# Stores of memory keys and output gates on the sync queue, seven staging tiles for keys, and a tail pool cut into parts

## The chip, the cores and the metric

The kernel runs on one core of a Trainium2 chip. A core has five engines, each with its own instruction queue: TensorE (PE in the profile, with weight loads listed as PEld), VectorE (DVE), ScalarE (ACT), GpSimd (POOL) and SyncE (SP), which here only issues DMA transfers. ScalarE issues transfers too; the issues are listed as SPq and ACTq. The metric is the device time of one execution in microseconds (us).

## The reference, cut to what matters

One layer of a bidirectional encoder on a sequence of 2048 rows of width 1024, with 256 memory rows. All of it is float32:

```python
u = rms_norm(h); proj = u @ w_in                     # columns for hyena, q k, v, o, gates
hy = short_conv(proj[..., :1536])                    # width 3, centred
qk = silu(short_conv(proj[..., 1536:2560]))          # width 3, centred
y_hy = group_rms_norm(hyena(hy), 8)                  # 512 channels, long filters by FFT
y_ml = group_rms_norm(sigmoid(o) * mlstm(qk, v, gates), 4)   # 4 heads x 128, both directions
h = h + concat(y_hy, y_ml) @ w_out
x, m = rms_norm(h), rms_norm(mem)                    # mem: 256 rows
h = h + softmax((x @ xa_wq) @ (m @ xa_wk).T / 16) @ (m @ xa_wv) @ xa_wo   # by 4 heads of 256
h = h + relu(rms_norm(h) @ ff_w1) ** 2 @ ff_w2
out = rms_norm(h)
```

## The kernel before, in words

A float32 product is written as three products of a high and a low part: `mm3` (lines 357, 360, 361) multiplies high by high, low by high and high by low. `split` (line 368) makes the parts: the high one by a cast on ScalarE, the low one by a subtraction on VectorE.

The program runs in stages that are woven into each other. Up to some 1020 us the rows of x are normalised and projected (`sweep`), the Hyena filters are transformed and the first Hyena products run. `sweep` writes each block of 128 rows by 256 columns by a copy or a sigmoid into a staging tile "st" (3 tiles in turn) and stores it: values into `vd`, output gates into `od` (line 886, on ScalarE's queue). From some 1020 to 1185 us `memproj` prepares the cross-attention: the product of the key weights with the memory is multiplied by the query weights (`keys`, L709 to L718), and the values by the output weights (`values`, L720 to L730). Each result goes from PSUM by ScalarE into a staging tile "o" (the same three "st" tiles, L706), and from there to DRAM: 16 stores of keys `gd` (L718) and 32 of values `vw` (L730), 256 KB each, all issued by ScalarE. The end of the Hyena part (loads `a<-zg`, `a<-hy`, stores `yh<-a`) and the first chunks of the mLSTM (loads `qn`, `kk_t`, `va`, `cbn`, `kn`, `og`; products L1188, L1272, L1310, L1312; normalised rows stored as `ym`) run beside it.

Attention follows from some 1190 to 1700 us, woven with the other mLSTM chunks: for each of four blocks of 512 rows it loads the rows of `yh` and `ym` (L1452), turns them with TensorE (L1458), splits them into `act`, multiplies with the columns of `w_out` (L1383, weights `wh`, `wl`; the first columns go through tiles "we"), adds the rows of x (`acc`, L1485), and then goes on with the keys `gd` and values `vw`. The feed-forward part follows to the end.

Memory on the chip is given out in pools. `i_sb` holds what the input and Hyena stages need, the staging tiles among it; it is closed before attention, and `tail_open` puts one pool `t` in its place with the residual `acc`, the activations, the weights and four loading tiles "wn". A tile of a new pool waits for the work on whatever lay in the same place of a pool that is closed.

The order on each engine is made by a scheduler when the program is built, from the order in which the generators are woven; it is fixed when the kernel runs. Each transfer that SP or ScalarE issues gets one of eight completion semaphores in turn, common to both queues, so an issue waits for the landing of the transfer that had it before, eight transfers back. In the profile a wait of this kind is listed as a wait for the tile of that other transfer.

## Time and profile before

| | us |
|---|---|
| median of 3 runs | 3109.32 (3107.85 to 3111.45) |
| the profiled execution | 3110.14 |
| its span | 3108.4 |
| TensorE busy in the span | 3025.3 |

The granted clock of TensorE over the profiled execution is 0.99 of full speed. A row of a list of waits reads: engine and line, what it waited for, total, times, longest. A row of the timeline reads: start, duration, engine, line, operation, tiles with their shapes, and in brackets the idle time before it with what ended it. The tile names are those of the program: `wm` are weights of the memory projection, `o` and `kt` copies out of PSUM, `we` and `wn` loaded weights or rows, `ht` the output of a chunk.

### The profile page before, as it was taken

Reading aid. Unit: us, or ns where it says so; the run is one execution under the profiler, and the core shown is the slowest. Engines: PE = TensorE matmul, PEld = TensorE weight load, DVE = VectorE, ACT = ScalarE, POOL = GpSimd, SP = SyncE. Lnnn points to the kernel's source line nnn. Section 1 sums busy time; section 2 is a strip of 40 time slices with the busy share of each in tenths; the row PEclk is TensorE's granted clock in tenths of the full one; section 3 lists DMA queues with packets and bytes.
Section 4 is the critical chain, followed back from the end, with each engine's and each line's share of the span. In section 5 each row is a group of like instructions: output and inputs, shape, how many; then the busy total and the mean of one; then the engine's idle time right before and its main releaser. Section 6 shows DMA issues by size and latency. Waiting matters only on the chain.

```text
span 3108.4 us, 42926 instructions
## 1 busy us (share of the span) xinstructions
PE 3025.3 (97%) x14257; PEld 2374.5 (76%) x14257; DVE 1955.3 (63%) x3429; ACT 1497.7 (48%) x2931; POOL 1141.1 (37%) x802
## 2 busy tenths in 40 slices
PE   8999999999999998999999999999999999999998
PEld 6655667776676766888887888888888788888876
DVE  7865465446756456877664566657554676565696
ACT  6543466533656225565544455556555443333335
POOL 0122011200222333333132337766466375243693
PEclk9999999999999999999999999999999999999999
DMA  6654768576878996565476557657644565354435
GB/s 211 190 198 163 231 207 251 178 232 194 254 203 241 302 300 220 158 199 170 143 250 206 197 172 235 207 178 238 200 153 153 171 210 182 109 166 118 157 93 172
DMA packets 444102, 607.07 MB, mean 195 GB/s; under 512 B 38494, under 2 KB 248542, under 8 KB 442856
## 3 DMA queue, kind: packets, MB, share of 16 engines
q1 hardware_dynamic: 405988, 546.54, 55.2%
q10 hardware_dynamic: 37892, 57.79, 5.5%
q8 instruction: 113, 1.85, 0.2%
q14 instruction: 109, 0.89, 0.1%
HBM read 401.79 MB, written 202.41 MB: 194 GB/s over the span
## 4 chain that ended last, share of the span: by engine, by line
PE 55%; DVE 3%; DMA 1%; issue 1%; ACT 1%; POOL 0%; SPq 0%; DVEq 0%; POOLq 0%; ACTq 0%
PE mm L361 12%; PE mm L357 12%; PE mm L360 12%; PE hy L357 6%; PE hy L361 6%; PE hy L360 6%; DVE bl L1668 1%; PE hy L1310 1%; PE hy L1312 1%; DVE acc L1960 0%; PE hy L1458 0%; DVE acc L1994 0%; PE hy L1571 0%; DMA va<-vd 0%; PE hy L1272 0%
## 5 line engine op out<-in xcount | busy, mean ns | idle before, releaser
L1668 DVE TENSOR_TENSOR bl<-wr,bh 128x512 fp32r<-128x512 f32 x213 | 242.1, 1142 | 127.6 <-ACT bh L1667 122.9
L1667 ACT CAST ah<-w 128x512 fp32r<-128x512 f32 x284 | 176.5, 622 | 301.1 <-PE hy L360 155.9
L368 DVE TENSOR_TENSOR wl<-wn,wh 128x512 fp32r<-128x512 f32 (+1 forms) x296 | 213.1, 765 | 101.0 <-ACT wh L368 100.4
L357 PE MATMUL mm<-xh,wh 128*128 128x512 f32 x640 | 267.5, 419 | 8.5 <-ACT wh L368 7.9
L1024 POOL TENSOR_TENSOR b<-b,a 128x512 f32<-128x512 f32 x64 | 87.0, 1362 | 509.4 <-ACT b L1022 238.8
L360 PE MATMUL mm<-xl,wh 128*128 128x512 f32 x640 | 253.7, 397 | 1.3 <-DVE xl L368 1.3
L361 PE MATMUL mm<-xh,wl 128*128 128x512 f32 x640 | 254.8, 399 | 0.0
L1667 ACT CAST bh<-wr 128x512 fp32r<-128x512 f32 x232 | 143.5, 621 | 230.2 <-PE mm L361 172.6
L1668 DVE TENSOR_TENSOR al<-w,ah 128x512 fp32r<-128x512 f32 x236 | 216.0, 916 | 55.5 <-ACT ah L1667 54.1
L357 PE MATMUL mm<-bh,ah 128*128 128x512 f32 x576 | 225.2, 391 | 1.8 <-DVE acc L1830 1.7
L361 PE MATMUL mm<-bh,al 128*128 128x512 f32 x576 | 223.3, 390 | 2.6 <-POOL al L1668 2.6
L360 PE MATMUL mm<-bl,ah 128*128 128x512 f32 x576 | 224.4, 390 | 0.0
L368 ACT CAST wh<-wn 128x512 fp32r<-128x512 f32 (+1 forms) x296 | 164.2, 618 | 109.4 <-PE mm L361 52.7
L360 PE MATMUL mm<-act,wh 128*128 128x512 f32 x512 | 202.3, 395 | 0.0
L361 PE MATMUL mm<-act,wl 128*128 128x512 f32 x512 | 200.5, 393 | 0.9 <-DVE wl L368 0.9
L357 PE MATMUL mm<-act,wh 128*128 128x512 f32 x512 | 199.6, 396 | 1.3 <-ACT wh L368 1.2
L357 PE MATMUL hy<-bh,ah 128*128 128x512 f32 x448 | 175.2, 391 | 0.0
L360 PE MATMUL hy<-bl,ah 128*128 128x512 f32 x448 | 174.6, 390 | 0.0
L361 PE MATMUL hy<-bh,al 128*128 128x512 f32 x448 | 174.4, 390 | 0.0
L357 PEld LDWEIGHTS mm<-xh,wh 128*128 128x128 f32 x640 | 121.1, 189 | 60.8 <-issue 18.6
L357 PE MATMUL mm<-wh,xh 128*128 128x256 f32 (+1 forms) x512 | 156.0, 305 | 3.8 <-ACT xh L368 2.3
L361 PEld LDWEIGHTS mm<-xh,wl 128*128 128x128 f32 x640 | 121.0, 189 | 47.8 <-issue 23.2
(375 smaller groups left out, 8225.4 us busy)
## 6 DMA issues: line engine op xcount, KB each, us to landing
wr<-hc SPq DMA_DIRECT2D x224, 256.0 KB
w<-in_ff_w_dram SPq DMA_DIRECT2D x172, 256.0 KB
hc<-wn SPq DMA_DIRECT2D x128, 256.0 KB
wn<-in_w_in_dram SPq DMA_DIRECT2D x100, 256.0 KB
hc<-q SPq DMA_DIRECT2D x96, 256.0 KB
fs<-a SPq DMA_DIRECT2D x32, 512.0 KB
a<-fs SPq DMA_DIRECT2D x64, 256.0 KB
a<-zs SPq DMA_DIRECT2D x64, 256.0 KB
```

What stands on the lines that cost most here:

```text
L357: first = mm(ps, lh, rh, start=start, stop=False)
L360: mm(ps, lh, rl, start=False, stop=False)
L361: self.last = mm(ps, ll, rh, start=False, stop=stop)
L368: both = (self.nc.scalar.copy(hi, src), self.nc.vector.tensor_tensor(lo, src, hi.bitcast(F32), ALU.subtract))
L1024: nc.gpsimd.tensor_tensor(xt, xt, hi[:, m], ALU.mult)
L1310: nc.tensor.matmul(dst, nm[:, h], va[:, h], start=True, stop=state is None)
L1312: nc.tensor.matmul(dst, rows_[d, 1][:, h], state[:, h], start=False, stop=True)
L1667: self.nc.scalar.copy(hi, src)
L1668: eng.tensor_tensor(lo, src, hi.bitcast(F32), ALU.subtract)
```

## The change

The change has four parts. The input pool is cut in three, `i_w` (tiles "cv" and "wn"), `i_st` (the three "st") and the rest, and the tail pool in four, which lie over them one by one: `t_w` (the first pair of weights), `t_acc` (`acc`), `t` (one pair of activations, the second pair of weights) and `t_n` (the other activations and the loading tiles). The staging of keys takes the three "st" tiles and the four "wn" tiles by turns. The 16 stores of keys, and 16 of the 32 stores of output gates, are issued by SP. And one chunk of the mLSTM fewer is written ahead of attention; attention's first two steps and two of the mLSTM are written by turns before the two are woven as before.

```diff
+        sw = self.isw = es.enter_context(tc.tile_pool(name="i_w", bufs=1))
+        for tag, n, bufs in (("cv", 1088, 2), ("wn", 544, 4)):
+            for _ in range(bufs):
+                sw.tile([128, n], F32, tag=tag, name=tag, bufs=bufs)
+        self.ist = es.enter_context(tc.tile_pool(name="i_st", bufs=1))
         sb = self.isb = es.enter_context(tc.tile_pool(name="i_sb", bufs=1))
...
-        def staged(p):
-            o = sb.tile([128, 2, 256], F32, tag="st", name="o", bufs=3)
+        def staged(p, wide=False):
+            if wide:
+                o = self.isw.tile([128, 2, 256], F32, tag="wn", name="o", bufs=4)
+            else:
+                o = self.ist.tile([128, 2, 256], F32, tag="st", name="o", bufs=3)
             nc.scalar.copy(o, p)
...
-                nc.scalar.dma_start(out=gd[h // 2, :, 2 * i2:2 * i2 + 2, cs], in_=staged(p))
+                nc.sync.dma_start(out=gd[h // 2, :, 2 * i2:2 * i2 + 2, cs], in_=staged(p, i2 % 2 == 0))
...
-                nc.scalar.dma_start(out=(self.d_vd if c2 < 2 else self.d_od)[r0:r0 + 128, 256 * (c2 % 2):256 * (c2 % 2) + 256],
-                                  in_=so)
+                (nc.sync if c2 == 2 else nc.scalar).dma_start(
+                    out=(self.d_vd if c2 < 2 else self.d_od)[r0:r0 + 128, 256 * (c2 % 2):256 * (c2 % 2) + 256], in_=so)
...
     def tail_open(self, es):
-        T = self.T = es.enter_context(self.tc.tile_pool(name="t", bufs=1))
-        self.acc = T.tile([128, 8, 512], F32, name="acc")
+        def pool(name):
+            return es.enter_context(self.tc.tile_pool(name=name, bufs=1))
+
+        self.wp = [pool("t_w"), None]
+        for tag in ("wh", "wl"):
+            self.wp[0].tile([128, 8, 256], F32R, tag=tag, name=tag)
+        self.acc = pool("t_acc").tile([128, 8, 512], F32, name="acc")
+        self.wp[1] = self.ap = pool("t")
         self.acts = 2
         for _ in range(2):
             self.act_tile("act")
         for tag in ("wh", "wl"):
-            for _ in range(2):
-                T.tile([128, 8, 256], F32R, tag=tag, name=tag, bufs=2)
-        self.acts = 0
+            self.wp[1].tile([128, 8, 256], F32R, tag=tag, name=tag)
+        self.T = pool("t_n")
+        self.acts = self.wps = 0
...
+    def pair(self, names):
+        pool = self.wp[self.wps % 2]
+        self.wps += 1
+        return [pool.tile([128, 8, 256], F32R, tag=t, name=n) for t, n in zip(("wh", "wl"), names)]
...
-                             p.turned_in(), take(n, 2), beside_each(n, take(m, 5)))
+                             p.turned_in(), take(n, 2), beside_each(n, take(m, 4)))
...
                 g = p.attention(at)
+                for x in (g, m, g, m):
+                    next(x)
                 weave(g, m, 440, 112, True)
```

The numbers of instructions on TensorE, VectorE and GpSimd stay as they are; 32 transfers go from ScalarE to SP. The line numbers of the changed kernel are 8 to 17 higher than those of the kernel before from the staging of keys on. In the rows that follow, a number at the end (x2) counts like instructions in a row.

ScalarE's queue among the keys, before: each copy of a product (L706) has its store behind it, and brm (a scale of the Hyena part) and kt (the next projected weights) stand among them.

```order
L718 DMA gd<-o 128x2x256
L213 ACTIVATE brm<-ms,eps 128x16
L701 COPY kt<-mm 128x512
L706 COPY o<-mm 128x512
L718 DMA gd<-o 128x2x256
L706 COPY o<-mm 128x512
```

The sync queue at the same place, after: the stores stand between the Hyena loads and stores and the weights wm.

```order
L1064 DMA yh<-a 64x1024 x2
L726 DMA gd<-o 128x2x256
L417 DMA wm<-in_xa_wq_t_dram 128x1024 x2
L969 DMA a<-zg_2628 128x1024 x2
L972 DMA a<-hy 64x1024 x2
L417 DMA wm<-in_xa_wv_dram 128x4x256 x2
L726 DMA gd<-o 128x2x256 x2
L1064 DMA yh<-a 64x1024 x2
```

On ScalarE only the copies, brm and kt are left; every store is now one of the issues that the loads behind it on SP wait for.

The sync queue at the start of attention, before: the first columns of w_out (we) are asked for early, then chunk loads, then the four row loads (wn<-yh), and va and the residual acc behind them.

```order
L1383 DMA we<-in_w_out_dram 128x2x256 x2
L1166 DMA kn<-kn 128x512
L1166 DMA og<-od 128x512
L1346 DMA ym<-ht 128x512 x2
L1247 DMA qn<-qt 128x4x128
L1247 DMA kk_t<-kt 128x4x128
L1172 DMA va<-vd 128x4x128
L1247 DMA cbn<-cbd 128x516
L1166 DMA kn<-kn 128x512
L1452 DMA wn<-yh 128x512 x4
```

The same queue after.

```order
L1469 DMA wn<-yh 128x512 x4
L1401 DMA we<-in_w_out_dram 128x2x256 x2
L1255 DMA cbn<-cbd 128x516
L1180 DMA va<-vd 128x4x128
L1174 DMA kn<-kn 128x512
L1401 DMA we<-in_w_out_dram 128x2x256 x2
L1502 DMA acc<-in_x_t_dram 128x4x512 x2
L1174 DMA og<-od 128x512
L1255 DMA qn<-qt 128x4x128
L1255 DMA kk_t<-kt 128x4x128
L1354 DMA ym<-ht 128x512 x2
L1180 DMA va<-vd 128x4x128
```

The row loads now come first, the weights behind them, and the second va load stands behind the two acc loads and the two ym stores.

VectorE at the start of attention, before: the low parts of the weights (wl), then the denominators (den) of the chunk that TensorE waits for.

```order
L1282 TENSOR_TENSOR rw<-rw,hy 128x512 x2
L1263 STREAM_SHUFFLE rw<-rows_9569 128x512 x2
L368 TENSOR_TENSOR wl<-we,wh 128x512 x3
L1173 MEMSET va 128x4
L1263 STREAM_SHUFFLE rw<-rows_9569 128x512 x2
L368 TENSOR_TENSOR wl<-we,wh 128x512
L1318 TENSOR_TENSOR den<-hy,cols 128x4 x2
L1319 RECIPROCAL den<-den 128x4 x2
```

After: a chunk's output (L1334) stands between the low parts, and the normalisation of a pair of chunks (from L216 on, ending in L1352 further down) right behind them.

```order
L368 TENSOR_TENSOR wl<-we,wh 128x512
L1334 SCALAR_TENSOR_TENSOR ht<-hy,den,ht 128x128 x4
L368 TENSOR_TENSOR wl<-we,wh 128x512 x3
L216 TENSOR_SCALAR hy<-brm 128x8
L218 COPY bry<-hy 128x8
L219 TENSOR_TENSOR hy<-hy,bry 128x8
L220 SCALAR_TENSOR_TENSOR hy<-hy,brm 128x8
```

The denominators no longer stand behind all four low parts, but the normalisation does.

More of the change, by code (lines that the diff above doesn't have):

```diff
@@ L390, in weights @@
                     cs = slice(c0, c0 + 512)
-                    nat = pool.tile([128, 512], F32, tag="wn", name="wn", bufs=nbufs)
+                    nat = self.isw.tile([128, 512], F32, tag="wn", name="wn", bufs=nbufs)
                     nc.sync.dma_start(out=nat, in_=w[128 * k0:128 * k0 + 128, cs])
@@ L395, in weights @@
         for k0 in range(0, kt, kc):
-            nat = pool.tile([128, kc, n], F32, tag="wn", name="wn", bufs=nbufs)
+            nat = self.isw.tile([128, kc, n], F32, tag="wn", name="wn", bufs=nbufs)
             nc.sync.dma_start(out=nat, in_=w[128 * k0:128 * (k0 + kc), :].rearrange("(k p) c -> p k c", p=128))
@@ L465, in square_sum @@
     def square_sum(self, x, dst):
-        junk = self.isb.tile([128, 512], F32, tag="st", name="junk", bufs=3)
+        junk = self.ist.tile([128, 512], F32, tag="st", name="junk", bufs=3)
         return self.tc.keep_in_program_order(self.nc.scalar.activation(junk, x, AF.Square, accum_out=dst))
@@ L530, in room @@
                 return None
-            t = self.isb.tile([128, 1088], F32, tag=("P", "cv")[n % 2], name="xt", bufs=2)
+            t = (self.isb, self.isw)[n % 2].tile([128, 1088], F32, tag=("P", "cv")[n % 2], name="xt", bufs=2)
             return t[:, 0:D].rearrange("p (k t) -> p k t", k=2)
@@ L578, in squares @@
             for k in range(8):
-                sq = sb.tile([128, 512], F32, tag="st", name="sq", bufs=3) if k else ssum[c]
+                sq = self.ist.tile([128, 512], F32, tag="st", name="sq", bufs=3) if k else ssum[c]
                 pin(nc.scalar.activation(sq, xs[k], AF.Square))
@@ L611, in second @@
             for k in range(0, 8, 2):
-                nat = sb.tile([128, 2, 256], F32, tag="wn", name="wn", bufs=4)
+                nat = self.isw.tile([128, 2, 256], F32, tag="wn", name="wn", bufs=4)
                 nc.sync.dma_start(out=nat, in_=wsrc1[:, k:k + 2])
@@ L787, in leave @@
                         ct = 2 * c2 + m
-                        cv = sb.tile([128, 1088], F32, tag="cv", name="cv", bufs=2)
+                        cv = self.isw.tile([128, 1088], F32, tag="cv", name="cv", bufs=2)
                         v = cv[:, 0:n]
@@ L835, in sweep_out @@
             pt = self.mm().rearrange("p (k t) -> p k t", k=4)
-            st = sb.tile([128, 4, 128], F32, tag="st", name="st", bufs=3)
+            st = self.ist.tile([128, 4, 128], F32, tag="st", name="st", bufs=3)
             full = min(4, (n - b) // 128)
@@ L880, in natural @@
                 self.pop()
-                so = sb.tile([128, 512], F32, tag="st", name="st", bufs=3)[:, 0:256]
+                so = self.ist.tile([128, 512], F32, tag="st", name="st", bufs=3)[:, 0:256]
                 if c2 < 2:
@@ L1369, in act_tile @@
         self.acts += 1
-        return self.T.tile([128, 8, 512], F32R, tag=f"act{(self.acts - 1) // 2 % 2}", name=name, bufs=2)
+        return (self.ap if (self.acts - 1) // 2 % 2 else self.T).tile([128, 8, 512], F32R, tag="act", name=name, bufs=2)
+    def pair(self, names):
+        pool = self.wp[self.wps % 2]
+        self.wps += 1
+        return [pool.tile([128, 8, 256], F32R, tag=t, name=n) for t, n in zip(("wh", "wl"), names)]
     def act(self):
@@ L1375, in columns @@
     def columns(self, w, stage=None):
-        hi = self.T.tile([128, 8, 256], F32R, tag="wh", name="wh", bufs=2)
-        lo = self.T.tile([128, 8, 256], F32R, tag="wl", name="wl", bufs=2)
+        hi, lo = self.pair(("wh", "wl"))
         n = 512 // w.shape[2]
@@ L1685, in ffn_x @@
     def ffn_x(self, i, src):
-        nc, T = self.nc, self.T
+        nc = self.nc
         eng = (nc.vector, nc.gpsimd)
@@ L1691, in ffn_x @@
         if i in (7, 3):
-            hi, lo = (T.tile([128, 8, 256], F32R, tag=t, name="x" + t[1], bufs=2).rearrange("p (k n) c -> p k (n c)", n=2)
-                      for t in ("wh", "wl"))
+            hi, lo = (t.rearrange("p (k n) c -> p k (n c)", n=2) for t in self.pair(("xh", "xl")))
         else:
```

11 lines of the change are left out of this document (5 added, 6 removed).

## The prediction

> **What bounds the kernel now.** First the page, for each engine's share of the span.
>
> ```profile
> span 3108.4 us, 42926 instructions
> PE 3025.3 (97%) x14257; PEld 2374.5 (76%) x14257; DVE 1955.3 (63%) x3429; ACT 1497.7 (48%) x2931; POOL 1141.1 (37%) x802
> ```
>
> TensorE works for all but 83.1 us. The change adds and removes no matmul, so all that it can win lies in those 83 us and in the stretches in which TensorE ran below full clock. Second, therefore, a table by stretches, cut where the change moves work: stretch, length, busy time of PE, PEld, DVE, ACT and POOL, granted clock, DMA share, GB/s. The last two rows are the slow-clock pieces of the stretch 1190 to 1220.
>
> ```profile
> 1060.00:1080.00 20.00, 15.62 (x55) 11.39 (x56) 6.74 (x21) 2.84 (x6) 4.38 (x3) 0.83 1.04 339
> 1080.00:1100.00 20.00, 20.00 (x95) 14.89 (x94) 10.52 (x31) 3.13 (x6) 5.69 (x5) 1.00 1.06 369
> 1100.00:1130.00 30.00, 25.09 (x108) 18.87 (x107) 14.03 (x40) 5.64 (x15) 12.22 (x9) 0.89 1.05 348
> 1130.00:1180.00 50.00, 49.80 (x221) 32.43 (x219) 26.82 (x92) 22.18 (x72) 18.96 (x15) 1.00 0.74 246
> 1190.00:1220.00 30.00, 16.95 (x90) 15.37 (x89) 22.48 (x63) 17.30 (x63) 9.45 (x8) 0.77 0.81 268
> 1330.00:1350.00 20.00, 15.60 (x80) 12.81 (x79) 14.09 (x32) 14.73 (x45) 1.60 (x2) 0.83 0.53 151
> 1350.00:1690.00 340.00, 339.83 (x1733) 286.65 (x1732) 229.38 (x524) 176.54 (x451) 96.22 (x70) 1.00 0.57 188
> ...
> 1197.05:1203.87 6.82, 2.94 (x13) 2.94 (x14) 5.25 (x16) 2.30 (x8) 4.20 (x3) 0.51 1.07 373
> 1207.35:1214.20 6.85, 5.05 (x22) 4.95 (x23) 6.57 (x23) 3.72 (x7) 0.00 (x0) 0.50 0.68 224
> ```
>
> Three places lose time: A (1060 to 1130, the keys of the memory projection), B (1190 to 1220, the handover to attention) and C (1330 to 1350, inside attention). Between 1350 and 1690 nothing can be won. A loses 4.38 + 4.91 = 9.3 us idle and by the clock 20 x 0.17 + 30 x 0.11 = 6.7 us more: 16.0 us. B loses 13.05 us idle and half of the 7.99 us that it was busy at half clock, 4.0 us: 17 us. C loses 20 - 15.60 = 4.4 us idle and up to 20 x 0.17 = 3.4 us by the clock.
>
> Third, who waits in A: the waits of TensorE, of ScalarE and of the sync queue from 1020 to 1140 (total, times, longest).
>
> ```profile
> PE mm L716 <- ACT o L706: 3.4, 2, 3.1
> PE mm L716 <- ACT kt L701: 2.4, 1, 2.4
> PE mm L699 <- ACT o L706: 2.0, 1, 2.0
> PE hy L1310 <- DVE a L1052: 1.8, 1, 1.8
> ...
> ACT o L706 <- DMA wm<-in_xa_wq_t_dram: 11.9, 3, 7.6
> ACT o L706 <- DMA wm<-in_xa_wo_dram: 10.1, 1, 10.1
> ...
> SPq L1056 <- DMA a<-zg: 7.8, 4, 3.0
> ```
>
> TensorE waits for ScalarE's copies out of PSUM, and ScalarE waits for loads that its copies never read: a store on ScalarE's queue must have its completion semaphore back from the transfer eight issues earlier, and that was a weight load on the sync queue. The timeline of the longest case, and two rows for the lead of the sync queue over TensorE:
>
> ```profile
> 1094.58 0.59 ACT L706 COPY o<-mm 128x512 f32<-128x512 f32 x1
> ...
> 1104.78 0.37 ACTq L718 DMA_DIRECT2D gd<-o  x1
> 1105.24 0.59 ACT L706 COPY o<-mm 128x512 f32<-128x512 f32 x1 [10.07 <-DMA wm<-in_xa_wo_dram]
> ...
> 1105.88 8.36 PE L716 MATMUL mm<-kt,wm 128*128 128x256 f32 x24 [3.07 <-ACT o L706]
> ...
> 1083.11 0.80 SPq L961 DMA_DIRECT2D a<-zg  x2
> ...
> 1097.22 0.64 PE L178 MATMUL hy<-a,e 128*64 128x512 f32 x1
> ...
> 1041.54 7.07 PE L716 MATMUL mm<-kt,wm 128*128 128x256 f32 x32
> ```
>
> The copy at 1094.58 was done at 1095.2, its store left at 1104.78, and the next copy, for which TensorE stood, came behind it.
>
> Fourth, B: the timelines of the queues and engines from 1164 to 1214, in the order of the argument.
>
> ```profile
> 1179.37 0.37 ACTq L730 DMA_DIRECT2D vw<-o  x1
> ...
> 1186.63 0.41 ACTq L730 DMA_DIRECT2D vw<-o  x1
> ...
> 1192.17 2.18 ACT L368 CAST wh<-we 128x512 fp32r<-128x512 f32 x4 [0.30 <-DMA vw<-o]
> ...
> 1200.28 1.12 ACT L1324 ACTIVATE ht<-hy,den 128x128 f32<-128x128 f32 x4
> ...
> 1204.09 1.28 ACT L1182 ACTIVATE ve<-va,cols 128x129 f32<-128x129 f32 x4 [2.69 <-DMA va<-vd]
> ...
> 1164.65 2.06 SPq L1383 DMA_DIRECT2D we<-in_w_out_dram  x2
> ...
> 1192.09 1.75 SPq L1452 DMA_DIRECT2D wn<-yh  x4
> ...
> 1195.99 1.36 SPq L1172 DMA_DIRECT2D va<-vd  x1
> ...
> 1177.72 2.22 DVE L1344 SCALAR_TENSOR_TENSOR ht<-ht,hy,gml 128x128 f32<-128x128 f32 x8
> ...
> 1193.27 3.70 DVE L368 TENSOR_TENSOR wl<-we,wh 128x512 fp32r<-128x512 f32 x3
> ...
> 1198.15 1.46 DVE L368 TENSOR_TENSOR wl<-we,wh 128x512 fp32r<-128x512 f32 x1
> ...
> 1200.93 2.09 PE L1188 MATMUL hy<-ve,kn 128*128 128x129 f32 x8 [7.58 <-ACT ht L1324]
> ...
> 1209.15 1.12 PE L1458 MATMUL hy<-ident,wn 128*128 128x128 f32 x4 [4.30 <-DVE act L368]
> ```
>
> The last vw store leaves at 1186.63 and has landed by 1192.09, 5.5 us later; only then does the one tail pool open, since it overlies the staging tile of that store. So the row loads start at 1192.09 and the first weight cast at 1192.17, though the weights were asked for at 1164.65. The four low parts hold VectorE from 1193.27 to 1199.6 and stand ahead of the state chunk's denominators: TensorE waits 7.58 us. Behind the blocked row loads the next va load leaves only at 1195.99; ve and then ScalarE's casts of the turned rows follow it: another 4.30 us.
>
> **The change, part by part.** *The 16 gd stores to the sync queue, seven staging tiles for three.* ScalarE loses 16 x 0.37 = 5.9 us of issue and, what counts, the 22.0 us for which its copies stood behind stores. The sync queue gains the 5.9 us and, for each store, a wait for its copy; behind it there stand the hyena loads (a<-zg, a<-hy), yh and the wm weights, and their reader is TensorE. What covers this is the lead: a row of a<-zg left at 1083.11 for a product at 1097.22, 14.1 us ahead. With seven tiles a copy waits for the landing of the store seven back, not three. If nothing else came, all of A's 16.0 us would return. But A runs at the limit of its transfers: DMA share 1.04 to 1.06. The stretch 1060 to 1130 moved 339 x 20 + 369 x 20 + 348 x 30 = 24.6 MB; at the best rate of the table, 369 GB/s, that takes 66.7 us, so with the same bytes inside it, only 3.3 us return. Loads may slide into 1130 to 1180 though, where 246 GB/s left room, and that by up to the lead. Between 3.3 and 16.0 I take the middle, 10 us: the lead of 14.1 us is of the size of the gap, but not all loads have it.
>
> The Trainium skill's page "DMA: Bandwidth & Descriptors", section "Issuing engines are not separate DMA queues", says that transfers issued from different engines run interleaved on the same 16 DMA engines, so that spreading them over issuers saves just the issue time. By that rule the move would be worth no more than the issue time, which lies beside other work here. The trace agrees on the shared engines (share over 1) but shows 22.0 us of waiting on ScalarE besides the issue; whether that returns, no run here shows yet.
>
> *The 16 od stores to the sync queue.* They are issued in the input sweeps, before 1020, where TensorE waits for none of them: 16 x 0.37 us on a queue that waits for its transfers anyway. Zero; ends -1 and +2.
>
> *The pools in parts, and the first turns between chunks 3 and 4.* By the changed order the row loads no longer stand behind va and kn of the next chunks, and their staging tiles no longer overlie those of the vw stores; they wait only for completion semaphores, and leave when the third-last vw store has landed, which in this trace is 1179.37 + 5.5 = 1184.9 instead of 1192.09. That is the gain. The price: the four weight loads, which left from 1164.65 on before, now stand behind the row loads. Four row loads take 1.75 us to issue; the first weights leave at 1186.6 and, with the same 5.5 us, are there at 1192.1: the first cast stays where it was. The second pair stands behind a kn load, and the third cast behind ve. The casts are then spread out and VectorE is done with the low parts some 3 us sooner. But behind them there now stand, on both engines, the sums (junk, brm), the 13 small steps of the normalisation and the 2.22 us of L1344, and TensorE's next chunk waits for these and for the ym store of the same tile, which takes another 5.5 us to land; the va load of chunk 4 comes behind that store. 3 us sooner, then 2.22 + 5.5 = 7.7 us more in the chain, against some 5 us less since the row loads, the turns and the acc loads are out of the way. I put B at 0. Ends: -12 (both waits, 7.58 + 4.30, gone) and +8 (the 7.7 us come on top).
>
> *C.* The row that waits there:
>
> ```profile
> 1335.85 2.10 PE L1458 MATMUL hy<-ident,wn 128*128 128x128 f32 x8 [4.40 <-DMA wn<-yh]
> ```
>
> The loads of the second column block's rows wait for four staging tiles that the low-part casts free; they have that wait in the changed order too. Zero, ends -4.4 and +4.4 (the wait gone, or doubled, since chunks and loads come at other places).
>
> *The feed-forward part*, from 1710, has the same rows in the same order: zero.
>
> **The sum.** The profiled execution took 3110.14 us, 1.7 us more than its span and 0.8 us over the median of 3109.32. 3109.3 - 10 (A) + 0 (B) + 0 (C) = 3099.3; I say 3099. One measurement of this kernel can tell some 0.2%, 6.2 us, from no change.
>
> **Rivals.** *The sync queue becomes the bound in A (slower).* Each of the 16 stores costs it 0.37 us and at most one product's time of waiting for its copy, 7.07 / 4 = 1.77 us: 34.2 us. Less the lead of 14.1 us, hyena's products would be late by up to 20.1 us, with none of A won; half of it, 10 us, gives 3119. It decides from (14.1 - 5.9) / 16 = 0.51 us of extra waiting for each store. For it speaks that this queue already waits for transfers nearly all the time (the row of 7.8 us is one of many); against it, that those waits and the stores' are for the same landings and do not add up.
>
> *The transfers bound A whoever issues them.* Then 3.3 us return: 3106. For it: the share over 1. Against it: the room after 1130. That is also the case in which the change does not do what it says. The rule of the Trainium skill's page quoted above speaks for a time near this one.
>
> *The handover's chain grows by its 7.7 us*, and A's 10 us are nearly eaten: 3109.3 - 10 + 8 = 3107. For it: the order; against it: the loads in front are fewer.
>
> *Both places empty out*: 3109.3 - 16 - 12 = 3081. For it: each wait named here hangs on the one thing removed. Against it: something is always late next, and DMA at its limit in A.
>
> **How the numbers follow.** My forecast, with its own range of 3092 to 3103, gets 0.42; both places empty 0.12; the transfers as bound 0.15; the longer handover 0.11; the sync queue as bound 0.20. The range from 3083 to 3119 leaves out about half of the first and half of the last of these rivals, 0.16. Faster by over 0.2% (under 3103.1): nearly all of the forecast, the empty case and a little of the two small ones, 0.56. Within 0.2%: most of those two, 0.22. Slower: the sync queue, and some of a worse handover, 0.22.
>
> **What would show it.** Right: from 1060 to 1130 no wait of TensorE for o or kt, no slow clock there, ScalarE without waits for wm; row loads of yh ahead of the last vw store's landing; the wait for ht at the handover replaced by one of about the same size for the normalisation, or for va. Wrong: TensorE waiting for a<-zg, a<-hy or wm in A (the sync queue), TensorE still idle there with DMA share at 1.05 (transfers), idle time in B over 20 us or under 6 us, a new wait between 1350 and 1710 for the vw or w_out weights, whose loads then stand closer to those of the feed-forward part.

## The result: slower, where a gain was forecast

| | before, us | after, us |
|---|---|---|
| median of 6 runs each | 3110.36 (3107.85 to 3111.58) | 3124.02 (3118.88 to 3129.37) |
| the profiled execution | 3110.14 | 3129.37 |
| its span | 3108.4 | 3127.6 |

The ratio is 1.0045 (1.0033 to 1.0057): the change costs 13.7 us. The profiled execution is the slowest of its six, 5 us over their median, so of its 19.2 us over the profiled execution before some 14 are the change. The page of the changed kernel, shares of the span:

```profile
span 3127.6 us, 42953 instructions
PE 3031.2 (97%) x14257; PEld 2377.3 (76%) x14257; DVE 1954.8 (63%) x3429; ACT 1501.8 (48%) x2931; POOL 1144.1 (37%) x802
```

The stretches of the changed kernel, in the columns of the table of before (length, busy PE, PEld, DVE, ACT, POOL, granted clock, DMA share, GB/s):

```profile
1060.00:1080.00 20.00, 19.11 (x85) 14.47 (x83) 10.94 (x32) 4.42 (x9) 6.67 (x6) 1.00 1.06 346
1080.00:1100.00 20.00, 16.82 (x75) 12.11 (x76) 7.45 (x19) 2.27 (x5) 4.68 (x4) 0.91 1.06 328
1100.00:1130.00 30.00, 30.00 (x134) 21.75 (x131) 14.16 (x38) 4.61 (x9) 11.30 (x8) 1.00 1.04 363
1130.00:1180.00 50.00, 45.51 (x178) 28.35 (x176) 21.11 (x66) 19.44 (x58) 16.40 (x13) 0.93 0.77 244
1190.00:1220.00 30.00, 20.79 (x117) 18.52 (x116) 24.66 (x73) 16.05 (x58) 12.14 (x10) 0.74 0.68 225
1220.00:1330.00 110.00, 103.04 (x575) 89.15 (x574) 86.75 (x246) 62.87 (x203) 39.57 (x30) 0.98 0.50 154
1350.00:1690.00 340.00, 328.79 (x1639) 275.84 (x1638) 228.94 (x514) 170.77 (x438) 89.91 (x63) 0.98 0.55 177
...
1184.70:1205.20 20.50, 10.54 (x45) 9.81 (x46) 14.54 (x50) 9.86 (x36) 6.29 (x5) 0.50 0.75 259
```

The loss among the keys (1060 to 1130) fell from 16.0 us to 4.07 idle + up to 1.8 by the clock. But 1130 to 1180, which lost 0.2 us, now loses 4.49 idle + up to 3.5 by the clock; 20.5 us of the handover run at half clock; and 1350 to 1690, full before, is idle for 11.2 us.

Since work slides between fixed stretches, the account below is cut at products instead: for each stage, the idle time between TensorE's matmuls, plus half of the time that matmuls ran at half clock, worked out from all the matmuls of the trace. Half, because matmuls in a row start twice as far apart there (the products mm<-mt,wm of the kernel after every 427 ns instead of 216).

| lost, us | before | after |
|---|---|---|
| keys (first key product to first value product) | 15.9 | 6.1 |
| values (to the last value product) | 0.2 | 6.1 |
| handover (to attention's first product act by wh) | 17.7 | 21.5 |
| rest of attention's first block | 0.3 | 8.6 |
| second block | 6.7 | 5.7 |
| third block and fourth block's turns | 0.0 | 10.2 |
| all other stages | 40.9 | 38.7 |
| sum | 81.7 | 96.9 |

15.2 of the 19.2 us stand in it. The keys won 9.8 us. The values and the handover gave that back (+5.9, +3.8), and the first and the third block added 8.3 and 10.2. The account is of the slowest execution, so its sizes are somewhat above those of the medians.

TensorE's waits of the changed kernel, first from 1020 to 1175 and then from 1175 to 1260 (total, times, longest):

```profile
PE hy L178 <- DMA a<-zg: 3.4, 2, 3.1
PE hy L1196 <- ACT ht L1332: 3.3, 1, 3.3
PE mm L724 <- DMA wm<-in_xa_wq_t_dram: 0.9, 2, 0.5
PE mm L704 <- ACT o L714: 0.4, 1, 0.4
...
PE hy L1318 <- ACT rw L1289: 5.6, 1, 5.6
PE hy L1318 <- DVE ht L1352: 5.1, 2, 3.6
PE hy L1318 <- DVE hy L220: 4.2, 1, 4.2
PE hy L1280 <- DVE act L368: 3.3, 2, 1.9
PE hy L1196 <- ACT ht L1332: 2.7, 1, 2.7
```

The waits for o and kt among the keys are all but gone (0.4 us). In their place TensorE waits 3.4 us for a<-zg and 0.9 us for wm, small, but the sign that the prediction had named for its rival of the sync queue. In the second list every wait is one of an mLSTM chunk (L1196, L1280, L1318), for the normalisation (L220, L1352), for ht, for rw and for the low parts of act.

The wait of 3.3 us for ht lies among the values. The timeline of the changed kernel there, ScalarE and TensorE:

```profile
1131.62 0.38 ACTq L738 DMA_DIRECT2D vw<-o  x1
1132.09 0.59 ACT L714 COPY o<-mm 128x512 f32<-128x512 f32 x1 [12.09 <-DMA a<-zg]
...
1134.18 1.14 ACT L1332 ACTIVATE ht<-hy,den 128x128 f32<-128x128 f32 x4 [0.44 <-DVE den L1327]
...
1134.86 2.09 PE L1196 MATMUL hy<-ve,kn 128*128 128x129 f32 x8 [3.29 <-ACT ht L1332]
```

This is the mechanism of the keys once more: the stores of values (16, not 32 as the description of the kernel before has it) stayed on ScalarE, and one of them, with the work behind it, stood 12.09 us for a transfer of the sync queue. The chunk's ht came behind it, though its last products had ended at 1131.15. TensorE's idle time and a half-clock piece from 1133.68 on make up the 6.1 us of the values. This is read from the trace alone, as no run moves the stores of values; where the chunk has another place (e9, e10 and e14 below) the values lose at most 2.2 us.

The timeline of the handover in the changed kernel, by queue and engine:

```profile
1176.76 1.86 SPq L1469 DMA_DIRECT2D wn<-yh  x4
...
1199.41 1.40 SPq L1354 DMA_DIRECT2D ym<-ht  x2
...
1184.85 0.62 ACT L368 CAST wh<-we 128x512 fp32r<-128x512 f32 x1 [4.24 <-DMA we<-in_w_out_dram]
1185.37 1.28 ACT L1289 ACTIVATE rw<-rw,cols 128x128 f32<-128x128 f32 x4
...
1197.46 1.28 ACT L1289 ACTIVATE rw<-rw,cols 128x128 f32<-128x128 f32 x4 [5.64 <-POOL rw L1287]
...
1174.70 2.31 PE L736 MATMUL mm<-wm,kt 128*128 128x512 f32 x5
...
1186.87 0.77 PE L1318 MATMUL hy<-va,rw 128*128 128x129 f32 x2 [5.57 <-ACT rw L1289]
...
1194.83 0.77 PE L1318 MATMUL hy<-va,rw 128*128 128x129 f32 x2 [4.18 <-DVE hy L220]
...
1200.50 0.80 PE L1318 MATMUL hy<-va,rw 128*128 128x129 f32 x2 [3.61 <-DVE ht L1352]
```

The row loads do leave early. But the next chunk's rw (1185.37) stands on ScalarE behind a cast that waited 4.24 us for its weights, and TensorE has nothing besides that chunk. Three waits of 3.6 to 5.6 us follow in a row.

The half-clock pieces of this trace last 3.41, 6.83 and, at this place, 20.48 us. The Trainium skill's page "TensorE: Matmul & The Clock Gate", section "Part 1: The HAM clock gate", says that the clock is set by windows of 3.41 us and falls to half after an idle one. The lengths agree, one, two and six windows, and in the window ahead of this piece, 1181.46 to 1184.88, no matmul ran. But the trace does not need an idle window: the piece at 1133.68 follows one in which TensorE was busy for 1.3 us, and this one stays at half while TensorE is busy for 10.54 of 20.50 us.

The third block, timeline of the changed kernel again:

```profile
1540.40 0.63 PE L1475 MATMUL hy<-ident,wn 128*128 128x128 f32 x4 [1.78 <-DMA wn<-ym]
...
1573.53 0.50 PE L357 MATMUL mm<-act,wh 128*128 128x512 f32 x1 [2.43 <-ACT wh L368]
...
1542.72 1.32 SPq L1679 DMA_DIRECT2D wr<-hg  x3
...
1547.85 5.16 SPq L1731 DMA_DIRECT2D w<-in_ff_w_dram  x4
...
1566.85 0.32 SPq L1401 DMA_DIRECT2D wn<-vw  x1
...
1557.55 0.62 ACT L1684 CAST ah<-wr 128x512 fp32r<-128x512 f32 x1 [3.17 <-DMA wr<-in_ff_w_dram]
...
1572.88 0.60 ACT L368 CAST wh<-wn 128x512 fp32r<-128x512 f32 x1
```

Loads for the feed-forward part (wr, w) and their casts on ScalarE (L1684, waiting 3.17 us) now stand among this block's loads of vw. Before, the first of them left later, though the whole kernel was ahead:

```profile
1559.59 1.76 SPq L1662 DMA_DIRECT2D wr<-hg  x4
```

### The profile page after: what moved, and what is told of

Read it like the earlier page. It is cut to its first block, busy times and chain, and to the rows that moved or that the text cites. A ratio compares the mean times of both kernels' runs of the same rounds, so it can differ in the third digit from the quotient of the medians.

```text
span 3127.6 us, 42953 instructions
## 1 busy us (share of the span) xinstructions
PE 3031.2 (97%) x14257; PEld 2377.3 (76%) x14257; DVE 1954.8 (63%) x3429; ACT 1501.8 (48%) x2931; POOL 1144.1 (37%) x802
## 4 chain that ended last, share of the span: by engine, by line
PE 81%; DMA 7%; DVE 6%; ACT 2%; issue 2%; POOL 1%; SPq 1%; ACTq 0%; DVEq 0%; POOLq 0%
PE mm L357 17%; PE mm L361 17%; PE mm L360 17%; PE hy L357 6%; PE hy L361 6%; PE hy L360 5%; PE hy L178 3%; PE mm L954 2%; PE hy L985 1%; PE hy L1027 1%; DMA a<-hy 1%; DMA a<-zg 1%; DVE bl L1685 1%; DMA va<-vd 1%; PE mm L827 1%
## 5 line engine op out<-in xcount | busy, mean ns | idle before, releaser
L1684 ACT CAST ah<-w 128x512 fp32r<-128x512 f32 x284 | 177.2, 625 | 302.0 <-PE hy L360 154.5
L368 DVE TENSOR_TENSOR wl<-wn,wh 128x512 fp32r<-128x512 f32 (+1 forms) x296 | 221.6, 793 | 115.8 <-ACT wh L368 115.2
L1684 ACT CAST bh<-wr 128x512 fp32r<-128x512 f32 x232 | 143.9, 623 | 228.0 <-PE mm L361 173.9
```

What stands on the lines that cost most here:

```text
L368: both = (self.nc.scalar.copy(hi, src), self.nc.vector.tensor_tensor(lo, src, hi.bitcast(F32), ALU.subtract))
L1684: self.nc.scalar.copy(hi, src)
```

## The experiments

Two theories to begin with. H: the handover's new order makes the loss, and the stores are a gain by themselves. S: the stores give their gain back at the handover whatever the order. P is the rival that the pools cost. Later ones: L, the feed-forward's early loads; N, the normalisation behind the casts; C, an mLSTM chunk that stands alone on TensorE costs some 9 us; Q, the queue and not the tiles is what helps the keys. "Stores" in the table are those of keys and gates, issued by SP; "tiles" are the seven staging tiles.

The results of all runs, with the account of the section before. "Alone" counts the chunks between the last value product and attention's first product. Ratios are to the kernel before on the same chip, with 95% intervals.

| run | keys + values | handover | alone | first two blocks | third block | sum | median, us | ratio |
|---|---|---|---|---|---|---|---|---|
| before | 16.1 | 17.7 | 2 | 7.0 | 0.0 | 81.7 | 3108.05 to 3110.36 | 1 |
| after | 12.2 | 21.5 | 2 | 14.3 | 10.2 | 96.9 | 3124.02 | 1.0045 (1.0033 to 1.0057) |
| e1 stores, tiles | 9.5 | 27.0 | 3 | 7.0 | 0.0 | 81.4 | 3111.27 | 1.0009 (0.9997 to 1.0021) |
| e2 pools | 17.5 | 15.4 | 2 | 6.1 | 0.4 | 77.8 | 3108.48 | 1.0002 (0.9993 to 1.0012) |
| e3 pools, order | 21.6 | 3.2 | 1 | 18.0 | 8.7 | 90.0 | 3120.49 | 1.0039 (1.0024 to 1.0053) |
| e4 stores, tiles, pools | 10.2 | 28.8 | 3 | 7.3 | 0.0 | 85.3 | 3111.75 | 1.0012 (1.0002 to 1.0021) |
| e5 after, one step less | 9.9 | 20.9 | 2 | 12.0 | 0.0 | 81.4 | 3110.47 | 1.0004 (0.9994 to 1.0015) |
| e6 e1, normalisation first | 10.6 | 26.4 | 3 | 6.6 | 0.2 | 78.3 | 3109.46 | 1.0002 (0.9992 to 1.0011) |
| e7 e5, normalisation first | 10.4 | 16.6 | 2 | 13.1 | 0.4 | 78.7 | 3106.52 | 0.9996 (0.9986 to 1.0005) |
| e8 keys' queue alone | 14.0 | 19.6 | 3 | 6.4 | 0.4 | 76.8 | 3107.11 | 1.0000 (0.9990 to 1.0009) |
| e9 e1, chunk first | 4.3 | 17.0 | 2 | 6.2 | 0.4 | 66.8 | 3094.80 | 0.9952 (0.9939 to 0.9966) |
| e10 e5, chunk first | 4.3 | 8.9 | 1 | 16.9 | 0.0 | 69.0 | 3092.98 | 0.9948 (0.9935 to 0.9961) |
| e11 after, three steps ahead | 10.4 | 14.3 | 1 | 20.0 | 0.0 | 83.2 | 3112.11 | 1.0005 (0.9996 to 1.0015) |
| e12 tiles alone | 9.2 | 27.2 | 3 | 6.6 | 0.0 | 80.1 | 3111.33 | 1.0007 (0.9997 to 1.0017) |
| e13 before, chunk first | 14.9 | 16.5 | 2 | 6.6 | 0.3 | 74.7 | 3105.17 | 0.9985 (0.9976 to 0.9994) |
| e14 after, chunk first | 3.9 | 9.7 | 1 | 20.2 | 11.7 | 83.5 | 3114.01 | 1.0011 (1.0001 to 1.0020) |
| e15 e12, chunk first | 16.8 | 16.9 | 2 | 7.2 | 0.3 | 78.0 | 3107.80 | 0.9996 (0.9987 to 1.0005) |

### The parts by themselves: e1 to e4

e1 is the kernel before with the stores of keys and gates on SP and seven staging tiles, all in the old pools (`staged`, as in the change but with tiles of the old pool, is not shown):

```diff
...
-                nc.scalar.dma_start(out=gd[h // 2, :, 2 * i2:2 * i2 + 2, cs], in_=staged(p))
+                nc.sync.dma_start(out=gd[h // 2, :, 2 * i2:2 * i2 + 2, cs], in_=staged(p, i2 % 2 == 0))
...
-                nc.scalar.dma_start(out=(self.d_vd if c2 < 2 else self.d_od)[r0:r0 + 128, 256 * (c2 % 2):256 * (c2 % 2) + 256],
+                (nc.sync if c2 == 2 else nc.scalar).dma_start(out=(self.d_vd if c2 < 2 else self.d_od)[r0:r0 + 128, 256 * (c2 % 2):256 * (c2 % 2) + 256],
```

> The kernel before with only the stores of keys and gates on the sync queue and seven staging tiles; pools and order of chunks as before. Theory H (the handover's new order makes the loss): stage A gains its 8 to 10 us, the handover is as before, 3101 us. Theory P (the pools in parts make the loss): the same, 3101. Theory S (the stores pay in the handover what they win among the keys): 3108 to 3125.

e2 is the kernel after with its stores on ScalarE, three staging tiles and the old order, so the pools alone; e3 has the new order too; e4 is the kernel after with the old order. The difference of e2 to the kernel after:

```diff
-                nc.sync.dma_start(out=gd[h // 2, :, 2 * i2:2 * i2 + 2, cs], in_=staged(p, i2 % 2 == 0))
+                nc.scalar.dma_start(out=gd[h // 2, :, 2 * i2:2 * i2 + 2, cs], in_=staged(p))
...
-                (nc.sync if c2 == 2 else nc.scalar).dma_start(
+                nc.scalar.dma_start(
...
-                             p.turned_in(), take(n, 2), beside_each(n, take(m, 4)))
+                             p.turned_in(), take(n, 2), beside_each(n, take(m, 5)))
...
-                for x in (g, m, g, m):
-                    next(x)
```

> The changed kernel with stores on ScalarE and three staging tiles as before, and five chunks ahead of attention without the four written steps: only the pools are in parts. Theory H: no loss, 3105 to 3112, with the two waits of the handover smaller. Theory P: the whole loss without the gain of the keys, some 3132. Theory S: 3105 to 3112.

The order of the kernel after with the stores of the kernel before (e3), difference to the kernel after:

```diff
-                nc.sync.dma_start(out=gd[h // 2, :, 2 * i2:2 * i2 + 2, cs], in_=staged(p, i2 % 2 == 0))
+                nc.scalar.dma_start(out=gd[h // 2, :, 2 * i2:2 * i2 + 2, cs], in_=staged(p))
...
-                (nc.sync if c2 == 2 else nc.scalar).dma_start(
+                nc.scalar.dma_start(
```

> Pools in parts and the changed order (four chunks ahead, the first steps by turns), stores as before. Theory H: the whole loss without the gain of the keys, 3130 to 3135. Theory P: the same. Theory S: no loss, 3105 to 3112.

The stores and pools in the old order (e4), difference to the kernel after:

```diff
-                             p.turned_in(), take(n, 2), beside_each(n, take(m, 4)))
+                             p.turned_in(), take(n, 2), beside_each(n, take(m, 5)))
...
-                for x in (g, m, g, m):
-                    next(x)
```

> Stores and pools as changed, order of chunks as before (five chunks ahead, no steps by turns). Theory H: 3095 to 3102, the gain of the keys and of the opened pool without the loss. Theory P: 3124, as the whole change. Theory S: 3115 to 3125.

The pools cost nothing that can be measured (e2), so P falls. By the ratios the order costs 12 us with the old stores (e3) and 10 with the new ones (after against e4), so H holds for the loss. But its other half fails: the stores are no gain, in either set of pools (e1, e4), as S says. S fails in its turn at e3, where it saw no loss (3105 to 3112, measured 3120.49). e3 lies between the ranges, and e4 (3111.75) under that of S: the loss of the order and the one behind the stores are two things. e3 shows too that the order can do at the handover more than the 12 us of the prediction's best end (17.7 to 3.2 us), and that the blocks behind take it all back (7.0 to 18.0, 0 to 8.7).

Where e1 gives its gain back: TensorE's waits in e1 from 1160 to 1235.

```profile
PE hy L1313 <- DVE bry L218: 9.3, 1, 9.3
PE hy L1461 <- DVE act L368: 4.8, 1, 4.8
```

The first value product came 17.2 us earlier than before and the last one 13.8, yet attention's first product 1.9 us later. Among the values e1 loses 6.4 us, mostly by the same wait as the kernel after (TensorE 3.7 us for ht, a copy on ScalarE 12.5 us behind a store of values). The handover loses 9.3 us more than before. The reason is the schedule: one chunk of the mLSTM that stood ahead of the last value product now stands behind it (three chunks ahead instead of four, three alone instead of two). Nothing in the edit names that chunk; the scheduler set it there.

### One step less, and the normalisation: e5 to e7

Six mLSTM steps are written before the weave in the kernel after (four, and two in the new loop), where there were five. e5 takes one away:

```diff
-                for x in (g, m, g, m):
+                for x in (g, m, g):
```

> The changed kernel with three written steps instead of four (attention, mLSTM, attention), so the mLSTM ends and the feed-forward part's first loads start one step later. Theory L (the 10.2 us that the changed kernel loses behind the first turns of the third block come from those loads): that loss is gone, 3112 to 3116. Rival (it comes from the pools or from the weave as such): 3121 to 3126, with the loss where it was.

e6 is e1, and e7 is e5, with the weight casts, and the ve copies of the next chunk, held behind the normalisation of the first pair of chunks (an order on the engines, with no wait added); of the edit this shows the casts:

```diff
...
-            self.split(hi[:, k0:k0 + n], lo[:, k0:k0 + n], nat)
+            self.split(hi[:, k0:k0 + n], lo[:, k0:k0 + n], nat, behind=self.first if stage else None)
```

> The stores alone (as in e1), and on ScalarE and VectorE the first pair's normalisation (junk, brm, L216 on, L1344) put ahead of the first weight casts and of the ve copies of the next chunk, nothing else. Theory N (the handover loses the gain of the keys because the normalisation stands behind casts and ve): of the wait of 9.3 us the 5 us go that these took in the row, and their share of the slow clock: 3102 to 3106. Rival (the chain is as long anyhow, the wait only changes its name): 3109 to 3113.

> The whole change with both edits, three written steps and the normalisation ahead of the casts. If L and N both hold and add up: 3103 to 3110. L alone: 3112 to 3116. N alone: 3115 to 3119. Neither: 3121 to 3126.

By the ratios (1.0045 and 1.0004) the step is worth 13 us, nearly all of the change's loss. The third block's loss goes from 10.2 to 0; the first block loses 10.5 us instead of 8.6, the second 1.5 instead of 5.7. The time, 3110.47, is a little under L's range of 3112 to 3116. e7 lies in the range set for L and N together, but only 4 us under e5, within the intervals of the two. N does not explain the handover: in e6 the wait for bry only moved, as TensorE's waits of e6 from 1160 to 1235 show.

```profile
PE hy L1199 <- ACT ht L1335: 7.5, 2, 7.1
PE hy L1473 <- DVE act L372: 4.5, 1, 4.5
PE hy L1321 <- DVE bry L218: 4.4, 1, 4.4
```

The handover loses 26.4 us instead of 27.0 (e7: 16.6 instead of 20.9). Whatever stands first, a chunk alone has its whole chain to go through.

### The chunk, the queue and the tiles: e8, e9, e12, e13, e15

e8 moves the stores of keys to SP with the three tiles kept:

```diff
-                nc.scalar.dma_start(out=gd[h // 2, :, 2 * i2:2 * i2 + 2, cs], in_=staged(p))
+                nc.sync.dma_start(out=gd[h // 2, :, 2 * i2:2 * i2 + 2, cs], in_=staged(p))
```

> The kernel before with only the 16 stores of keys on the sync queue; three staging tiles, output gates on ScalarE. Theory Q (the queue makes the gain among the keys): the loss from the first keys product to the last values product falls from 16.1 to under 10 us as in e1 (9.5). Rival (the seven tiles make it): it stays at 14 or more. The total follows the handover: 3100 to 3112.

e9 is e1, with each chunk written ahead of a step of the memory projection instead of behind it:

```diff
 def beside_each(g, h):
+    yield next(h, 0)
     for v in g:
-        yield v
         yield next(h, 0)
+        yield v
     yield from h
```

> The stores alone (as in e1), but each mLSTM chunk written ahead of a step of the memory projection instead of behind it, so that in the order on TensorE two chunks and not three stand between the last values product and attention's first product. Theory C (each bare chunk costs some 9 us of its own latency; in the runs so far 1 chunk 3, 2 chunks 15 to 22, 3 chunks 20 to 29 us): the handover loses about 18 us instead of 27, the keys keep their gain, 3100 to 3104. Rival (the handover is held by its transfers and casts, whatever the chunks): 3109 to 3113.

e12 has the seven tiles (`staged`, as in e1, is not shown), with all stores left on ScalarE:

```diff
...
-                nc.scalar.dma_start(out=gd[h // 2, :, 2 * i2:2 * i2 + 2, cs], in_=staged(p))
+                nc.scalar.dma_start(out=gd[h // 2, :, 2 * i2:2 * i2 + 2, cs], in_=staged(p, i2 % 2 == 0))
```

> The kernel before with only the seven staging tiles for keys; all stores on ScalarE. With e8 (queue alone, 14.0 us lost among the keys instead of 15.9): if the tiles alone make the gain, 6 us or less is lost there; if it takes both, 12 or more. The total follows the handover, which has three bare chunks: 3108 to 3114.

e13 is the kernel before, and e15 is e12, with the edit of e9:

> The kernel before with nothing but each chunk written ahead of a step of the memory projection; stores, tiles and pools as before, two chunks bare as before. Theory C (the gain of e9 is the gain of the keys, no longer given back): no change, 3106 to 3112, with 14 to 20 us lost among the keys. Rival (the chunks' place makes the gain by itself): 3093 to 3100.

> Seven staging tiles with all stores on ScalarE, chunks first. If the tiles make most of the gain: some 3 us above e9 (the keys lose 9.2 us in e12 against 9.5 in e1 with the values, 4.3 in e9): 3095 to 3100. If the queue is needed: 3104 to 3110.

With the chunk back ahead of the last value product, the stores keep their gain: e9 is at 3094.80, a ratio of 0.9952, below the 3100 to 3104 that C had given it. The edit of `beside_each` alone is worth 4.6 us (e13, a gain clear of noise where none was expected), the stores and tiles alone nothing (e1), the two together 14.4 us: with the chunk in its new place, stores and tiles are worth some 10 us. The stretch of the keys in e9, and TensorE's waits there:

```profile
1060.00:1130.00 70.00, 68.54 (x343) 53.17 (x343) 35.01 (x109) 22.07 (x73) 28.03 (x21) 1.00 1.05 351
```

```profile
PE mm L731 <- ACT o L709: 1.4, 1, 1.4
PE mm L699 <- ACT o L709: 0.8, 1, 0.8
```

TensorE is busy for 68.54 of 70 us at a DMA share of 1.05, so transfers at their limit did not bound this stage.

Queue or tiles: what ScalarE waits for from 1020 to 1140, in e8 (queue alone), in e12 and in e15 (tiles alone):

```profile
ACT o L706 <- DMA gd<-o: 42.4, 9, 10.2
```

```profile
ACT o L709 <- DMA a<-zg: 10.3, 2, 7.8
ACT o L709 <- DMA a<-hy: 8.2, 2, 4.3
ACT o L709 <- DMA wm<-in_xa_wq_t_dram: 7.7, 3, 3.4
```

```profile
ACT o L709 <- DMA wm<-in_xa_wv_dram: 9.7, 1, 9.7
...
ACT brm L213 <- DMA wm<-in_xa_wk_dram: 3.9, 1, 3.9
```

With three tiles on SP the copies wait 42.4 us for the landing of the store three back. With seven tiles on ScalarE they and brm wait for loads of the other queue, as before. Each edit alone moves the wait to the other cause. By e8 alone Q fails: 14.0 us are lost among keys and values, which was the rival's condition. e15 against e9 differs only in who issues the 32 stores, and that is 16.8 us against 4.3 among keys and values and 13 us in the whole: there Q holds, with tiles enough and the chunk first. With the chunk in its old place it does not: e12 and e1 differ in the same way and come out alike (9.2 and 9.5 us, 3111.33 and 3111.27). What the queue wins among the keys (e1 loses 3.1 us there, e12 7.4) is lost again among the values (6.4 and 1.8). Why e15 loses more there than e12 is not settled.

The page "DMA: Bandwidth & Descriptors" of the Trainium skill, section "Issuing engines are not separate DMA queues", holds that another issuer saves only the time of the issue. e8 (3107.11, no change) and e1 against e12 agree; e15 against e9 does not: there the issuer decides what stands behind a wait.

### The best version, and the step again: e10, e11, e14

e10 is e5, and e14 the kernel after, with the edit of e9. They differ in one mLSTM step of the loop:

```diff
-                for x in (g, m, g, m):
+                for x in (g, m, g):
```

> The whole change with three written steps (as in e5) and each chunk ahead of a step of the memory projection: one bare chunk. Theory C: the handover falls from 20.9 us to 3 to 10 us, of which the wait for ym behind it may keep some: 3095 to 3104. Rival: 3108 to 3112 as e5.

> The changed kernel with its four written steps, and nothing but each chunk ahead of a step of the memory projection. Theories C and L together: e10 (3093) plus the 9 to 10 us of the early feed-forward loads: 3100 to 3105. Without L: 3093.

e11 asks whether a chunk fewer ahead would do as well, difference to the kernel after:

```diff
-                             p.turned_in(), take(n, 2), beside_each(n, take(m, 4)))
+                             p.turned_in(), take(n, 2), beside_each(n, take(m, 3)))
...
-                for x in (g, m, g, m):
+                for x in (g, m, m, g):
```

> The whole change with three chunks instead of four ahead of attention and the steps attention, mLSTM, mLSTM, attention: the mLSTM ends as in e5, one chunk is bare ahead of the first product, the others come behind it and attention's second half of the first turns waits for their rows. Theory C: the handover falls to under 10 us, but the wait for ym grows by what was bare: 3103 to 3112. Rival: 3110 as e5.

e10 is the fastest of all, 0.9948 (0.9935 to 0.9961), 30 us under the kernel after and 2 us under the range of its theory; it can't be told from e9. e11 wins at the handover, though less than expected (14.3 us lost, not under 10), and loses it in the first block. The step that e14 has over e10 costs 20 us by the ratios, twice what its expectation gave it: 3114.01, not 3100 to 3105. The stretches 1340 to 1480 and 1480 to 1620, of e10 first and then of e14:

```profile
1340.00:1480.00 140.00, 139.53 (x748) 119.23 (x747) 108.24 (x258) 79.59 (x226) 53.27 (x38) 1.00 0.57 186
1480.00:1620.00 140.00, 139.87 (x692) 117.13 (x691) 96.42 (x204) 71.50 (x166) 37.66 (x26) 1.00 0.64 211
```

```profile
1340.00:1480.00 140.00, 135.86 (x721) 115.38 (x720) 103.94 (x261) 78.53 (x223) 47.34 (x34) 0.98 0.56 183
1480.00:1620.00 140.00, 133.18 (x627) 110.41 (x626) 88.99 (x165) 68.52 (x155) 37.64 (x26) 0.96 0.60 199
```

What the step does is seen from where the mLSTM ends. From the start of its last score product (qn by kk_t) to the third block's first turn it is 41.8 us in the kernel after, e3 and e14, 12.6 in e5, e7, e10 and e11, and 25.7 in the kernel before and all others. Just the three with 41.8 lose at the third block (10.2, 8.7, 11.7; every other at most 0.4). So the loss belongs to the mLSTM ending a step early against attention. That can act in two ways, and the runs do not part them: no chunk is left to fill TensorE's waits, or the feed-forward's loads and casts, which follow the mLSTM's end, stand in the way. The timeline of the kernel after has both: of its 7.0 us of idle time from 1480 to 1620, 3.8 are turns that wait for ym rows and act, with no feed-forward load ahead of those rows, and 3.2 are waits for wh and act casts, behind such loads and casts. What e10 loses instead stands in the first block, TensorE's waits from 1160 to 1235:

```profile
PE hy L1475 <- DMA wn<-ym: 9.0, 2, 8.2
PE hy L1475 <- DMA wn<-yh: 5.0, 2, 3.6
```

The second half of the first block's rows are outputs of chunks that have only just been written. That would be the next thing to win; it wasn't tried.

Theory C, over all the runs: with one chunk alone the handover loses 3.2 to 14.3 us, with two 15.4 to 21.5, with three 19.6 to 28.8. The groups overlap a little, but one chunk more or less is of the size of the whole gain of the stores. The cleanest pairs are e1 and e9 (27.0 to 17.0 us) and e12 and e15 (27.2 to 16.9), which differ only in the place of the chunks, and before and e13, where the number alone stays at two (17.7 and 16.5). The count is not the whole: one chunk alone is paid for in the first two blocks, and with them the runs with one lose 21.2 to 34.3 us, those with two 21.5 to 35.8.

## Why the prediction was wrong

*A, 10 us from the stores: the cause right, the size partly luck.* The keys won 9.8 us, the waits for o and kt went, and the slow clock is down to one piece. The reason given, that a store on ScalarE's queue waits for foreign loads, is shown by e15 against e9. The middle was taken for a doubt about transfers that did not come true: e9 says that some 12 us are there (16.1 to 4.3 with the values), at the same DMA share. So the transfers were no bound. SP was none in the main, but 3.4 us of waits for a<-zg and 0.9 for wm stood among the keys of the kernel after; in e9 0.7 us for a<-zg are left.

*What was left out of A: what the faster keys do to the schedule.* The prediction let the gain run through to the end with B at its own price. In fact the values, with their own stores still on ScalarE, lost 5.9 us that they had not lost before. And where the order was left as it was, a chunk that had stood ahead of the last value product went behind it and cost the handover 9.3 us (e1, with no other part of the change). e9 puts that chunk back, and the gain comes through. This is the first step that failed: the gain was credited in full, with nothing for what faster keys do to the stages behind them.

*"I put B at 0": the mechanism right, the size wrong.* The row loads left early, at 1176.76, and the first cast stands 7.8 us behind the last value product (7.6 before), so it did stay where it was against the work in front. The chain through the normalisation is there too (4.2 and 5.1 us). But the account had it beside other work: it measured +3.8 in the handover and +8.3 in the rest of the first block, above the upper end of +8 together. What was not counted is that TensorE has only the chunk to do, so that each of its links is a wait and the clock falls for 20.5 us. In the first block it is the same: 6.9 us of its 8.6 are waits of chunks for L1352, ht and act from 1228 to 1275, the rest a half-clock piece.

*C, 0: right within its ends* (6.7 to 5.7 for the second block).

*"Between 1350 and 1690 nothing can be won": true, and beside the point.* Nothing was counted as to be lost there either, since the order of the feed-forward's rows was the same. The edit's extra mLSTM step cost 10.2 us in the third block, worth with its other effects nearly the whole loss (e5: 13 us). The prediction's last paragraph had named a new wait between 1350 and 1710, for weights behind the feed-forward's loads, as a sign of error; the wait of 2.43 us for wh at 1573.53 is it, though it is less than half of that loss. This step gave the sign of the result.

*The od stores and the pools at 0*: the pools are shown (e2); the od stores (the last left at 1027.6 us, not before 1020) were never tried alone, and the stages ahead of the keys lost 28.4 us before and 29.6 after.

Of the rivals, the one on the slower side (3119) came nearest in time, by luck: its cause, the sync queue, accounts for a few us at most; the longer handover (3107) had a true cause and credited A's gain in full.

## What to carry to other kernels

Where a scheduler orders woven chains, a faster stage changes which filler stands in it: before crediting a gain, see whether the recurrent work stays ahead of the next handover, and pin it there by the order in which it is written. A queue and its staging tiles are one resource: moving a store to another engine without tiles, or adding tiles without moving the store, each won nothing in the whole, and the two together some 10 us, but only once the chunk was pinned. Look also at the stores of the next stage: those that stay on the old queue can take the gain back. Count the steps of the filler that an edit writes early, since a step that goes ahead is missing at the far end of the weave.

## What was not expected of the hardware

TensorE was busy for 98% of the keys' stretch at a DMA share of 1.05 (e9), with 351 GB/s and so less than the 369 GB/s of the best stretch before: a share above 1 was no sign of the bound. And three waits of 3.6 to 5.6 us in a row came with a granted clock of 0.50 for 20.5 us, in which TensorE was busy for 10.54 us, with matmuls that start twice as far apart as at full clock.

How much work keeps the clock up can be read from the 17 traces, cut into the windows of 3.41 us at which the clock steps. From 30 us on, a window at full clock was followed by half clock only where TensorE was busy for at most 1.74 us of it, and by full clock only where it was busy for at least 1.45. A window at half clock was followed by half clock only up to 2.75 us busy, and by full clock only from 2.79 on. So a row of waits can halve the clock though no window is idle, as at 1133.68.
